# A two-layer macaron transformer on one core: the token mixer's attention in a written order that three engines keep

## The chip, the core and the metric

The kernel runs on one core of a Trainium2 chip. The metric is the device time of one execution in microseconds (us), as the median of several runs. A difference of about 0.3% (3 us here) is what a measurement of this kernel can tell from no change.

The core's engines are called PE (matrix products; PEld are its weight loads), DVE (vector), ACT (activation functions), POOL and SP (which issues the loads). Each works through its own list of instructions in order and waits at an instruction until what it needs has been done on the other engines.

## The reference

Two layers, each a half-weighted gated FFN, a token mixer and a second half-weighted gated FFN, on 256 tokens of width 1024, in fp32:

```python
for l in range(DEPTH):
    x = x + FFN_RES_WEIGHT * swiglu_ffn(x, ffn1_norm[l], ffn1_w1[l], ffn1_w3[l], ffn1_w2[l])
    h = rms_norm(x, mix_norm[l])
    (fq, fk, fv, ff, gu, gv, nq, nkc, nvc, nks, nvs, nkw, nvw, ng, pz) = split_mixing_columns(h @ w_in[l])
    ...
    o_a = fox_mixer(...)      # 4 heads, softmax(q k / 8 + c_i - c_j), c the running sum of log sigmoid(ff)
    o_b = gmlp_mixer(...)     # gelu(u) * (causal 128x128 mix of normalized gelu(v))
    o_c = nsa_mixer(...)      # 4 heads on one KV head: compressed, selected and window branch, gated
    o_d = pool_mixer(...)     # causal averages over 2, 4, 8, 16 tokens, then a 64x64 product
    x = x + jnp.concatenate([o_a, o_b, o_c, o_d], axis=-1) @ w_out[l]
    x = x + FFN_RES_WEIGHT * swiglu_ffn(x, ffn2_norm[l], ffn2_w1[l], ffn2_w3[l], ffn2_w2[l])
```

With 256 tokens the NSA selection takes all four blocks and the window spans everything, so those two branches are plain causal attention over different keys and values.

## The kernel before

All products with weights are made in two parts to keep fp32 precision: a matrix is loaded (L109), its rounded part `h` is made by ACT (L112) and the rest `lo` by DVE (L113). Such a pair is called a split here. `mm3` (L133 to L135) makes a product from three passes, `mm2` (L139, L140) from two. One 128x2048 weight tile is split in two halves of 128x1024, or in four of 128x512 for the first tiles of an FFN. Four tiles hold loaded weights (`raws`), four pairs hold split ones (`spl`), eight PSUM banks hold products.

An FFN is a loop over 22 up tiles and 8 down columns of 22 products each; PE works there without a break. The mixer is a list of calls (L820 to L888) whose steps are short and depend on each other:

- projections A, U, D, C, B, Z (`project`, `u_proj`, `z_proj`), each with its splits;
- six attention jobs of one pair of heads: F0 and F1 (forget attention), N0 to N3 (two pairs by two branches of NSA). A job is `scores` (8 products L750; DVE adds the mask and takes the maximum, L758; ACT takes exponentials and sums, L760), `weights` (DVE inverts the sums, L766 and L768, and scales the rows, four times L772; PE transposes, six times L775; ACT copies them out, L777) and `values` (8 products, L787);
- the compressed branch: `cmp_hidden` (four calls, L444), `cmp_gelu`, `cmp_out`, `cmp_keys`, `cmp_scores` (L707, then the sum with the mask on DVE, L710, and a softmax), `cmp_weights` (L732); its product with the values is L793 in `done`;
- the gate (`gate_mix`, L550 to L558) and the pools (`pool_mix`, `pool_out`; L593, evacuated by L127 on ACT and L128 on DVE);
- the output projection `out_part`: four generators w00, w01, w10, w11 of 16 steps with 3 products each, called in pieces by `fill` between the other steps.

The order of the calls is not the order on the engines: a list scheduler works out, when the kernel is built, which ready instruction each engine takes next, from its own estimate of times. What comes out is a fixed list for each engine. The call order serves as priority. So a split whose tile is loaded is put wherever the scheduler thinks ACT and DVE are free, also between the steps of a job.

"Attention" below is the stretch from the running sums of the forget gate (`forget_sums`, L663) to `done`; "layer 0" and "layer 1" are its two occurrences.

Of the kernel before, what the change touches and what calls it, by code (L numbers as in the profile page):

```python
# [21 lines left out]
F32 = mybir.dt.float32  # L22
# [48 lines left out]
def tile_macaron(ctx, tc, xT, g0, const0, consts, params, w13, w2, wA, wB, wD, wC, wE, wcmp, wo, out):  # L71
# [27 lines left out]
    def halves(s):  # L99
        return s.rearrange("p (a n) -> p a n", a=2)  # L100

# [237 lines left out]
    def mixer(l, norm, par):  # L339
# [6 lines left out]
        e = SimpleNamespace()  # L346
# [10 lines left out]
        def project(wg, n):  # L357

            ps = [bank_a(), bank_a()]
            for q in range(2):  # L360
                h, lo = split(wg[q], 4 * n)
                for kk in range(4):
                    k = 4 * q + kk
                    s = slice(n * kk, n * kk + n)
                    for t in range(2):
                        tok = slice(128 * t, 128 * t + 128)
                        mm3(ps[t][:, :n], (xs[k][0][:, tok], xs[k][1][:, tok]), (h[:, s], lo[:, s]), k == 0, k == 7)
            return ps
# [34 lines left out]
        def a_proj():  # L403
            e.pA = project(wA[l], 384)
# [46 lines left out]
        def cmp_gelu():  # L451

            x = bank_h()[:, 0:64].rearrange("p (a h n) -> p a h n", a=2, h=2)[:, :, :, 0:NC]
            for a in range(2):
                for hb in range(2):
                    nc.tensor.matmul(x[:, a, hb, :], e.hid[a][:, 128 * hb:128 * hb + 128], C("stack")[:, 0:NC],
                                     start=True, stop=True)
            g = w1p.tile([128, 2, 2, 16], F32, name="g")[:, :, :, 0:NC]
            nc.scalar.activation(g, x, AF.Square)
# [3 lines left out]
            nc.scalar.activation(g, g, AF.Exp, scale=-1.5957691216057308)  # L463
            nc.vector.tensor_scalar(g, g, 1.0, None, op0=ALU.add)
# [10 lines left out]
        def cmp_out():  # L475
# [14 lines left out]
            kiv = inv_rms(kss[0:NC, :], 64, 1, NC)  # L490
            nc.vector.scalar_tensor_tensor(kcn[0:NC, 0:64], pkc[0:NC, 0:64], kiv, Pm("kcn", NC), op0=ALU.mult,
# [71 lines left out]
        def z_proj():  # L563
            h, lo = split(wE[l, 1], 2048)
            pz = halves(bank_h())
            for t in range(2):
                tok = slice(128 * t, 128 * t + 128)
                for k in range(8):
                    s = slice(256 * k, 256 * k + 256)
                    mm3(pz[:, t, :], (xs[k][0][:, tok], xs[k][1][:, tok]), (h[:, s], lo[:, s]), k == 0, k == 7)  # L570
            z = halves(s2())
            for t in range(2):
                nc.scalar.activation(z[:, t, :], pz[:, t, :], AF.Copy, scale=e.rstd[:, t:t + 1])
            e.z = z
# [23 lines left out]
        def b_proj():  # L598
            e.pB = project(wB[l], 384)
# [33 lines left out]
        def d_proj():  # L633
            e.pD = project(wD[l], 400)
# [35 lines left out]
        def fox_bias(pair):  # L670
# [10 lines left out]
            e.bias = [(b0[:, i, 0:128], b1[:, i, :]) for i in range(2)]  # L681


        def c_proj():
            e.pC = project(wC[l], 512)
# [16 lines left out]
        def cmp_scores():  # L702
# [11 lines left out]
            sc8 = sc.rearrange("p t h n -> p (t h) n")[:, :, 0:NC]  # L714
            cmx = wk.tile([128, 8], F32)
            nc.vector.tensor_reduce(cmx, sc8, op=ALU.max, axis=AX.X)
            nc.vector.tensor_tensor(sc8, sc8, cmx.unsqueeze(2).to_broadcast([128, 8, NC]), op=ALU.subtract)
            nc.scalar.activation(sc8, sc8, AF.Exp)
            csm = wk.tile([128, 8], F32)
# [22 lines left out]
        def scores(jb):  # L742

            q, ks = jb.qk()
            if jb.branch is None:
                fox_bias(jb.pair)
# [5 lines left out]
            bias = e.bias if jb.branch is None else [(mask[:, 128:256], mask)] * 2  # L752
# [10 lines left out]
        def weights(jb):  # L763
# [5 lines left out]
            jb.pT = []  # L769
            for i in range(2):  # L770
                for t, c in enumerate(tcols):
                    nc.vector.tensor_scalar(jb.s[i][:, c], jb.s[i][:, c], rv[:, t, i:i + 1], None, op0=ALU.mult)  # L772
                p = bank_h()
# [31 lines left out]
        def out_part(d, q, accs):  # L805

            h, lo = split(wo[l, d, q], 2048)
            for c, kk in [(c, kk) for k2 in (0, 2) for c in range(4) for kk in (k2, k2 + 1)]:
# [22 lines left out]
        c_proj()  # L831
        c_stats()
        forget_sums()
        b_proj()
        c_post()
        b_stats()
        cmp_hidden(0, 0)
        c_heads()
        scores(F0)
        b_post()  # L840
        z_proj()
        scores(F1)
        cmp_hidden(0, 1)
        weights(F0)
        gate_mix()
        cmp_hidden(1, 0)
        b_heads()
        pool_mix()
        values(F0)
        scores(N0)  # L850
        weights(F1)
        cmp_hidden(1, 1)
        pool_out()
        done(F0)
        scores(N1)
        cmp_gelu()
        values(F1)
        done(F1)
# [3 lines left out]
        weights(N0)  # L862
        fill(w00, 4)
        cmp_out()
        scores(N2)
        values(N0)
        fill(w00, 4)
        weights(N1)
        fill(w00)
        cmp_keys()  # L870
        scores(N3)
        values(N1)
        fill(w01, 4)
        weights(N2)
        cmp_scores()
        fill(w01, 4)
# [4 lines left out]
        weights(N3)  # L881
        fill(w10, 6)
        cmp_weights()
        fill(w10)
        values(N3)
        done(N1)
        done(N3)
        fill(w11, 8)  # L888

# [131 lines left out]
```

## Time and profile before

| | us |
|---|---|
| median of 3 runs | 983.67 (982.35 to 985.51) |
| the profiled execution | 980.94 |
| its span, first to last instruction | 979.2 |
| PE busy | 966.6 (99%) |
| DVE busy | 696.7 (71%) |
| ACT busy | 531.8 (54%) |
| weights and data loaded | 179.28 MB |

PE's busy time is a sum over pipelined products with modelled ends, so 99% does not mean that PE streams at full rate all the time; idle time of PE, and stretches in which its clock is lower, are read separately. The clock is granted at two levels, 1.2 and 2.4 GHz, shown as 0.50 and 1.00.

### The profile page before, as it was taken

The numbers are of one execution on the slowest core, as the hardware profiler recorded it, in microseconds if no ns is written. First come the engines' busy times: TensorE is split into PE (matmuls) and PEld (weight loads), VectorE is DVE, ScalarE is ACT, GpSimd is POOL, SyncE is SP. The second block draws the span as 40 slices with busy tenths as digits, with TensorE's granted clock in tenths as the row PEclk, the third lists the DMA queues.
The fourth block names the chain that finished last, engine by engine and source line by source line (L and its number), as shares of the span: only waits on it lengthen the run. The fifth ranks groups of instructions, "written<-read, shape, count | busy, mean of one in ns | idle before, by whom it ended". The sixth has DMA issues, their size and how long they took to land.

```text
span 979.2 us, 14917 instructions
## 1 busy us (share of the span) xinstructions
PE 966.6 (99%) x5840; PEld 840.3 (86%) x5840; DVE 696.7 (71%) x1256; ACT 531.8 (54%) x969; POOL 65.1 (7%) x67
## 2 busy tenths in 40 slices
PE   8999999999999999999999999999999999999998
PEld 6888888898779888888888888888987788888887
DVE  5988776575857777776668777665758587777751
ACT  6656555453746555654445655544537475565530
POOL 2000000032002000000010000001220030000000
PEclk9999999999979999999999999999999999999999
DMA  8975554535634655555545555545437255555530
GB/s 302 327 250 193 179 208 151 183 134 202 221 124 150 236 174 184 201 175 182 205 172 178 204 178 178 199 162 173 173 130 282 74 205 172 186 201 173 177 108 17
DMA packets 28150, 179.28 MB, mean 183 GB/s; under 512 B 3248, under 2 KB 5168, under 8 KB 8240
## 3 DMA queue, kind: packets, MB, share of 16 engines
q1 hardware_dynamic: 27792, 178.19, 52.3%
q8 instruction: 46, 0.75, 0.3%
q10 hardware_dynamic: 288, 0.14, 0.1%
q14 instruction: 24, 0.20, 0.1%
HBM read 177.27 MB, written 1.05 MB: 182 GB/s over the span
## 4 chain that ended last, share of the span: by engine, by line
PE 91%; ACT 3%; DMA 3%; DVE 3%; issue 1%; POOL 0%; SPq 0%; POOLq 0%
PE h L139 32%; PE a L139 17%; PE h L140 16%; PE a L140 8%; PE a L133 4%; PE a L135 4%; PE a L134 4%; DMA r<-in_wo_dram 2%; ACT h L112 1%; DVE lo L113 1%; DMA x<-in_xT_dram 1%; PE h L775 1%; PE a L787 1%; ACT s L760 1%; DVE s L758 0%
## 5 line engine op out<-in xcount | busy, mean ns | idle before, releaser
L113 DVE TENSOR_TENSOR lo<-r,h 128x1024 fp32r<-128x1024 f32 (+4 forms) x346 | 392.4, 1148 | 163.7 <-ACT h L112 163.0
L139 PE MATMUL h<-hl,h 128*128 128x512 f32 x1408 | 496.8, 398 | 1.7 <-ACT h L112 1.2
L112 ACT ACTIVATE h<-r 128x1024 fp32r<-128x1024 f32 (+4 forms) x346 | 328.6, 974 | 273.9 <-issue 227.1
L140 PE MATMUL h<-hl,lo 128*128 128x256 f32 x1408 | 395.0, 281 | 0.4 <-DVE lo L113 0.2
L139 PEld LDWEIGHTS h<-hl,h 128*128 128x128 f32 x1408 | 264.2, 188 | 66.4 <-ACT h L112 1.7
L140 PEld LDWEIGHTS h<-hl,lo 128*128 128x128 f32 x1408 | 265.8, 189 | 1.9 <-DVE lo L113 1.9
L139 PE MATMUL a<-hl,h 128*128 128x512 f32 x704 | 247.6, 397 | 0.0
L140 PE MATMUL a<-hl,lo 128*128 128x256 f32 x704 | 197.0, 280 | 0.0
L139 PEld LDWEIGHTS a<-hl,h 128*128 128x128 f32 x704 | 132.1, 188 | 32.6 <-DVE hl L125 1.0
L140 PEld LDWEIGHTS a<-hl,lo 128*128 128x128 f32 x704 | 132.8, 189 | 0.0
L224 DVE SCALAR_TENSOR_TENSOR x<-a,x 128x256 f32<-128x256 f32 x80 | 32.9, 421 | 51.7 <-PE a L140 46.0
L294 DVE TENSOR_TENSOR s<-h,s 128x256 f32<-128x256 f32 x176 | 66.0, 416 | 1.1 <-ACT s L293 1.1
L295 DVE TENSOR_TENSOR s<-s,rb 128x512 f32<-128x512 f32 x88 | 60.9, 692 | 2.8
L293 ACT ACTIVATE s<-h 128x256 f32<-128x256 f32 x176 | 56.5, 371 | 2.7 <-PE h L140 2.7
L124 ACT ACTIVATE hl<-s 128x256 fp32r<-128x256 f32 x92 | 38.2, 417 | 34.4 <-DVE s L298 34.2
L201 POOL TENSOR_TENSOR s<-s 128x512 f32<-128x512 f32 x12 | 16.8, 1399 | 594.9 <-ACT s L197 594.9
L297 ACT ACTIVATE s<-s 128x256 f32<-128x256 f32 x88 | 35.5, 403 | 17.9 <-DVE s L295 17.8
L133 PE MATMUL a<-h,hl 128*128 128x384 f32 (+2 forms) x128 | 45.2, 353 | 0.0
L135 PE MATMUL a<-h,hl 128*128 128x384 f32 (+2 forms) x128 | 44.9, 351 | 0.0
L134 PE MATMUL a<-lo,hl 128*128 128x384 f32 (+2 forms) x128 | 44.9, 351 | 0.0
L125 DVE TENSOR_TENSOR hl<-s,hl 128x256 fp32r<-128x256 f32 x92 | 38.4, 419 | 2.5 <-ACT hl L124 2.5
L298 DVE TENSOR_TENSOR s<-s 128x256 f32<-128x256 f32 x88 | 36.9, 419 | 3.4 <-ACT s L297 3.4
(186 smaller groups left out, 791.0 us busy)
## 6 DMA issues: line engine op xcount, KB each, us to landing
r<-in_w_dram SPq DMA_DIRECT2D x129, 1024.0 KB, 4.9
r<-in_wcmp_dram SPq DMA_DIRECT2D x8, 1024.0 KB, 4.8
r<-in_wo_dram SPq DMA_DIRECT2D x8, 1024.0 KB, 6.7
r<-in_wE_dram SPq DMA_DIRECT2D x4, 1024.0 KB, 5.0
r<-in_wC_dram SPq DMA_DIRECT2D x4, 1024.0 KB, 4.7
r<-in_wD_dram SPq DMA_DIRECT2D x4, 800.0 KB, 4.4
r<-in_wA_dram SPq DMA_DIRECT2D x4, 768.0 KB, 4.3
r<-in_wB_dram SPq DMA_DIRECT2D x4, 768.0 KB, 4.3
```

The source lines that it names most:

```text
L112: nc.scalar.activation(h[:, c], r[:, c], AF.Copy)
L113: nc.vector.tensor_tensor(lo[:, c], r[:, c], h[:, c].bitcast(F32), op=ALU.subtract)
L124: nc.scalar.activation(th, src, AF.Copy)
L125: nc.vector.tensor_tensor(tl, src, th.bitcast(F32), op=ALU.subtract)
L133: nc.tensor.matmul(o, wgt[0], mov[0], start=start, stop=False)
L134: nc.tensor.matmul(o, wgt[0], mov[1], start=False, stop=False)
L135: return nc.tensor.matmul(o, wgt[1], mov[0], start=False, stop=stop)
L139: nc.tensor.matmul(o, wgt[0], mov[2], start=start, stop=False)
L140: return nc.tensor.matmul(o[:, :T], wgt[1], mov[0], start=False, stop=stop)
L293: nc.scalar.activation(hr[:, j, :], st[m][j][:, T:], AF.Copy)
L294: nc.vector.tensor_tensor(hr[:, j, :], st[m][j][:, :T], hr[:, j, :], op=ALU.add)
L295: nc.vector.tensor_tensor(hr, hr, st["rb"].unsqueeze(1).to_broadcast([128, 2, T]), op=ALU.mult)
```

## The change

The mixer's call order from the running sums to the last output steps is rewritten, some steps are cut into pieces, and the order of the calls is made the order of the instructions on PE, DVE and ACT: `pin` links each instruction of this stretch to the one before it on its engine. SP and POOL are not linked, nor is what comes ahead of the stretch or behind it; instructions of the following FFN can still be placed between linked ones.

- `project`, `z_proj` and `out_part` first issue their splits and pause (`yield`), so the caller says at which place in the order the splits stand and where the products follow. In the old code B's products stood in one piece; now they come in quarters with other steps between.
- `weights` is cut into `scale` (DVE) and `trans` (PE transposes, ACT copies); a job's `scale` now stands with the next job's `scores`, before or after it, and its `trans` some steps later.
- `fox_bias` is called by itself; `cmp_gelu`, `cmp_out` and `cmp_scores` pause between their parts; `cmp_gelu` copies its product out of PSUM once (one more small ACT instruction), and `z_proj` uses one bank for each half of the tokens instead of one for both.

No product is added or removed: PE has as many instructions as before, ACT has two more in all, DVE as many.

```diff
+    def pin(start):
+        last = {}
+        for i in list(nc.cur_bb.bb.instructions)[start:]:
+            if i.engine in (mybir.EngineType.PE, mybir.EngineType.DVE, mybir.EngineType.Activation):
+                if i.engine in last:
+                    tc.add_manual_dep(i, last[i.engine], mybir.DependencyInfo(mybir.DependencyClass.NoSync,
+                                                                             mybir.DependencyReason.DATA), reason="pin")
+                last[i.engine] = i.name
...
+        def project(wg, n, ps):
+            hl = [split(wg[q], 4 * n) for q in range(2)]
+            yield
+            for k in range(8):
...
+                if k % 2:
+                    yield
...
-        def weights(jb):
+        def scale(jb):
...
+        def trans(jb):
...
         def out_part(d, q, accs):
             h, lo = split(wo[l, d, q], 2048)
+            yield
...
+        bq, zq = b_proj(), z_proj()
+        go = lambda gen: next(gen, None)
+        go(bq)
         c_stats()
         forget_sums()
+        here = len(nc.cur_bb.bb.instructions)
+        go(bq)
+        gate_mix()
+        go(bq)
+        go(zq)
+        cmp_hidden(0, 0)
         c_post()
+        fox_bias(0)
+        go(bq)
         c_heads()
...
+        done(F0)
+        trans(F1)
         fill(w00, 4)
+        go(gelu)
+        pool_out()
+        go(w01)
+        values(F1)
+        scale(N0)
+        scores(N1)
+        done(F1)
         fill(w00, 4)
+        go(gelu)
+        trans(N0)
+        fill(w00, 4)
+        values(N0)
+        scale(N1)
+        scores(N2)
         fill(w00, 4)
+        outs = cmp_out()
+        go(outs)
...
+        go(w10)
+        trans(N1)
+        fill(w01, 4)
+        go(outs)
+        values(N1)
+        scale(N2)
+        scores(N3)
+        fill(w01, 4)
+        trans(N2)
+        cmp_keys()
         fill(w10, 4)
         values(N2)
+        cs = cmp_scores()
+        go(cs)
+        go(w11)
+        scale(N3)
+        fill(w10, 4)
+        go(cs)
+        trans(N3)
+        fill(w10, 3)
+        go(cs)
+        fill(w10, 2)
         cmp_weights()
+        values(N3)
         fill(w10)
         done(N1)
         done(N3)
         fill(w11, 8)
+        pin(here)
```

Line numbers of the new kernel differ: L123 is the DVE half of a split (before L113), L122 its ACT half (L112), L793 the scaling (L772), L788 and L790 the inverted sums (L766, L768), L780 the masked maximum (L758), L782 the exponentials (L760), L800 the transposes (L775), L802 their copies (L777), L732 the masked compressed scores (L710), L137 and L138 the evacuation of the pools (L127, L128), L135 the DVE half of a finished head pair (L125).

The first place is DVE around the scaling of the last job, N3 (in the rows `rv` is the inverted sum, `s` a job's scores, `sc` the compressed scores, `lo<-r,h` a split). Before, layer 0:

```order
L766 RECIPROCAL rv<-sm 128x4
L768 TENSOR_TENSOR rv<-rv,gate 128x4
L772 TENSOR_SCALAR s<-s,rv 128x128
L772 TENSOR_SCALAR s<-s,rv 128x256
L710 TENSOR_TENSOR sc<-h,cst 128x8x15
L772 TENSOR_SCALAR s<-s,rv 128x128
L716 TENSOR_REDUCE cmx<-sc 128x8
L772 TENSOR_SCALAR s<-s,rv 128x256
```

Half of the scaling stands ahead of the masked compressed scores and no split between them. On DVE now:

```order
L732 TENSOR_TENSOR sc<-h,cst 128x8x15
L123 TENSOR_TENSOR lo<-r,h 128x1024 x2
L788 RECIPROCAL rv<-sm 128x4
L123 TENSOR_TENSOR lo<-r,h 128x512
L790 TENSOR_TENSOR rv<-rv,gate 128x4
L123 TENSOR_TENSOR lo<-r,h 128x512
L793 TENSOR_SCALAR s<-s,rv 128x128
L793 TENSOR_SCALAR s<-s,rv 128x256
L793 TENSOR_SCALAR s<-s,rv 128x128
L793 TENSOR_SCALAR s<-s,rv 128x256
```

The scaling of N3 now stands behind the masked compressed scores, both halves of w11's split and two quarters of the next FFN's first split.

The second place is DVE around the scaling of N0 (`hl<-h,par,hl` is the evacuation of the pools). Before, layer 0:

```order
L113 TENSOR_TENSOR lo<-r,h 128x1024 x2
L448 COPY s<-h 128x256
L766 RECIPROCAL rv<-sm 128x4
L768 TENSOR_TENSOR rv<-rv,gate 128x4
L128 SCALAR_TENSOR_TENSOR hl<-h,par,hl 128x256
L772 TENSOR_SCALAR s<-s,rv 128x128
L772 TENSOR_SCALAR s<-s,rv 128x256
L772 TENSOR_SCALAR s<-s,rv 128x128
L772 TENSOR_SCALAR s<-s,rv 128x256
```

Two halves of a split stand ahead of the scaling here too, but ahead of the pools' evacuations. On DVE now:

```order
L138 SCALAR_TENSOR_TENSOR hl<-h,par,hl 128x256 x2
L123 TENSOR_TENSOR lo<-r,h 128x1024 x2
L788 RECIPROCAL rv<-sm 128x4
L790 TENSOR_TENSOR rv<-rv,gate 128x4
L793 TENSOR_SCALAR s<-s,rv 128x128
L793 TENSOR_SCALAR s<-s,rv 128x256
L793 TENSOR_SCALAR s<-s,rv 128x128
L793 TENSOR_SCALAR s<-s,rv 128x256
```

The scaling of N0 now stands behind both evacuations of the pools and both halves of w01's split.

The third place is ACT from the evacuation of the pools to the copies of N0's transposed weights. Before, layer 0:

```order
L127 ACTIVATE hl<-h,par 128x256
L112 ACTIVATE h<-r 128x1024
L127 ACTIVATE hl<-h,par 128x256
L124 ACTIVATE hl<-a 128x256
L459 ACTIVATE g<-h 128x4x15
L112 ACTIVATE h<-r 128x1024 x2
L760 ACTIVATE s,sm<-s,nm 128x128
L760 ACTIVATE s,sm<-s,nm 128x256
L760 ACTIVATE s,sm<-s,nm 128x128
L760 ACTIVATE s,sm<-s,nm 128x256
L124 ACTIVATE hl<-a 128x256
L777 ACTIVATE s<-h 128x384 x2
```

On ACT now:

```order
L137 ACTIVATE hl<-h,par 128x256 x2
L122 ACTIVATE h<-r 128x1024 x2
L782 ACTIVATE s,sm<-s,nm 128x128
L782 ACTIVATE s,sm<-s,nm 128x256
L782 ACTIVATE s,sm<-s,nm 128x128
L782 ACTIVATE s,sm<-s,nm 128x256
L134 ACTIVATE hl<-a 128x256
L802 ACTIVATE s<-h 128x384 x2
```

The kinds of work and their sequence are much the same; which split it is has moved (two halves of w01 behind both evacuations), and so has what the exponentials wait for on DVE.

## Rows read from the trace of the kernel before

**Rows 1.** The profile page: TensorE's clock in 40 equal slices, in tenths of full speed.

```profile
PEclk9999999999979999999999999999999999999999
```

**Rows 2.** What PE waited for in layer 0's attention: us in total, times, longest.

```profile
PE h L775 <- DVE s L772: 1.6, 2, 1.3
PE h L750 <- ACT s L629: 0.6, 1, 0.6
PE a L787 <- ACT s L777: 0.5, 1, 0.5
```

**Rows 3.** The same for layer 1's attention.

```profile
PE h L775 <- DVE s L772: 1.7, 2, 1.3
PE a L787 <- ACT s L777: 0.4, 1, 0.4
```

**Rows 4.** Stretches with a low clock: length, then busy time by engine; PEclk third from last.

```profile
278.80:289.60 10.80, 10.44 (x50) 8.14 (x51) 7.26 (x33) 4.15 (x15) 0.00 (x0) 0.53 0.29 99
...
763.60:767.40 3.80, 3.80 (x18) 2.07 (x17) 2.85 (x15) 2.07 (x9) 0.00 (x0) 0.55 0.00 0
```

**Rows 5.** PE in order of time, layer 0: start, length; idle time before in brackets.

```profile
229.31 0.28 PE L663 MATMUL h<-lf,c0t 128*128 128x4 f32 x2
...
258.22 0.93 PE L750 MATMUL h<-s 64*128 64x128 f32 x8 [0.61 <-ACT s L629]
259.08 0.88 PE L775 MATMUL h<-c0t,s 128*128 128x128 f32 x6
...
264.81 0.28 PE L134 MATMUL a<-hl,h 128*128 128x256 f32 x1
264.93 0.28 PE L135 MATMUL a<-hl,lo 128*128 128x256 f32 x1
...
275.88 0.87 PE L787 MATMUL a<-s 128*64 128x256 f32 x8
276.68 0.55 PE L775 MATMUL h<-c0t,s 128*128 128x128 f32 x3
278.51 0.30 PE L775 MATMUL h<-c0t,s 128*128 128x128 f32 x1 [1.28 <-DVE s L772]
...
296.17 1.13 PE L793 MATMUL a<-pcT,vbd 128*128 128x256 f32 x4
```

**Rows 6.** PE in order of time, layer 1.

```profile
714.65 0.28 PE L663 MATMUL h<-lf,c0t 128*128 128x4 f32 x2
...
778.02 1.13 PE L793 MATMUL a<-pcT,vbd 128*128 128x256 f32 x4
```

**Rows 7.** DVE in order of time, layer 0.

```profile
254.24 0.75 DVE L555 TENSOR_TENSOR s<-h,par 128x256 f32<-128x256 f32 x2
...
260.30 2.35 DVE L113 TENSOR_TENSOR lo<-r,h 128x1024 fp32r<-128x1024 f32 x2
...
263.84 1.00 DVE L772 TENSOR_SCALAR s<-s,rv 128x128 f32<-128x128 f32 x4
264.76 0.48 DVE L128 SCALAR_TENSOR_TENSOR hl<-h,par,hl 128x256 fp32r<-128x256 f32 x1
...
284.02 0.17 DVE L766 RECIPROCAL rv<-sm 128x4 f32<-128x4 f32 x1
...
284.43 0.55 DVE L772 TENSOR_SCALAR s<-s,rv 128x128 f32<-128x128 f32 x2
...
296.07 1.90 DVE L113 TENSOR_TENSOR lo<-r,h 128x512 fp32r<-128x512 f32 x3 [6.83 <-ACT h L112]
```

**Rows 8.** ACT in order of time, layer 0.

```profile
256.50 0.71 ACT L124 ACTIVATE hl<-s 128x256 fp32r<-128x256 f32 x2
...
258.54 2.01 ACT L112 ACTIVATE h<-r 128x1024 fp32r<-128x1024 f32 x2
260.44 0.40 ACT L760 ACTIVATE s<-s,nm 128x128 f32<-128x128 f32 x1
...
262.19 0.86 ACT L777 ACTIVATE s<-h 128x384 f32<-128x384 f32 x2
```

More of the change, by code (lines that the diff above doesn't have):

```diff
@@ L569, in z_proj @@
                     s = slice(256 * k, 256 * k + 256)
[L570 to L574, printed above, removed]
+                    mm3(pz, (xs[k][0][:, tok], xs[k][1][:, tok]), (h[:, s], lo[:, s]), k == 0, k == 7)
+                nc.scalar.activation(e.z[:, t, :], pz, AF.Copy, scale=e.rstd[:, t:t + 1])
+                yield
         def pool_mix():
@@ L680, in fox_bias @@
             nc.vector.tensor_tensor(b1, p, mask.unsqueeze(1).to_broadcast([128, 2, 256]), op=ALU.add)
-            e.bias = [(b0[:, i, 0:128], b1[:, i, :]) for i in range(2)]
+            e.bias[pair] = [(b0[:, i, 0:128], b1[:, i, :]) for i in range(2)]
         def c_proj():
-            e.pC = project(wC[l], 512)
+            e.pC = projected(wC[l], 512)
         def c_stats():
@@ L744, in scores @@
             q, ks = jb.qk()
-            if jb.branch is None:
-                fox_bias(jb.pair)
             s = [bank_h(), bank_h()]
@@ L751, in scores @@
                                      start=True, stop=True)
-            bias = e.bias if jb.branch is None else [(mask[:, 128:256], mask)] * 2
+            bias = e.bias[jb.pair] if jb.branch is None else [(mask[:, 128:256], mask)] * 2
             jb.s = [s2(), s2()]
@@ L772, in weights @@
                     nc.vector.tensor_scalar(jb.s[i][:, c], jb.s[i][:, c], rv[:, t, i:i + 1], None, op0=ALU.mult)
+        def trans(jb):
+            jb.pT = []
+            for i in range(2):
                 p = bank_h()
@@ L843, in mixer @@
[L843 to L858, printed above, removed]
         wacc = [halves(bank_a()), halves(bank_a())]
         w00, w01 = out_part(0, 0, wacc), out_part(0, 1, wacc)
-        fill(w00, 4)
-        weights(N0)
-        fill(w00, 4)
@@ L864, in mixer @@
-        cmp_out()
+        go(w00)
+        go(bq)
+        cmp_hidden(0, 1)
+        b_stats()
+        scores(F0)
+        go(zq)
+        fox_bias(1)
+        cmp_hidden(1, 0)
+        scale(F0)
+        b_post()
+        scores(F1)
+        go(zq)
+        trans(F0)
+        b_heads()
+        cmp_hidden(1, 1)
+        pool_mix()
+        scale(F1)
+        scores(N0)
+        values(F0)
+        gelu = cmp_gelu()
+        go(gelu)
+        done(F0)
+        trans(F1)
+        fill(w00, 4)
@@ L865, in mixer @@
+        go(gelu)
[5 more added lines that the diff above has]
+        done(F1)
+        fill(w00, 4)
+        go(gelu)
+        trans(N0)
+        fill(w00, 4)
+        values(N0)
+        scale(N1)
         scores(N2)
-        values(N0)
         fill(w00, 4)
[L868 to L876, printed above, removed]
+        outs = cmp_out()
```

54 lines of the change are left out of this document (26 added, 28 removed).

## The prediction

> **What bounds the kernel now.** I looked at the clock row of the page first [rows 1]: full speed everywhere except around slices 11 and 12, and those slices lie in layer 0's attention. Then at what PE waited for inside the two attentions: 1.6 + 0.6 + 0.5 = 2.7 us in layer 0 [rows 2] and 1.7 + 0.4 = 2.1 us in layer 1 [rows 3], 4.8 us in all. Then at the clock in short stretches [rows 4]: 10.8 us at a mean of 0.53 in layer 0, 3.8 us at 0.55 in layer 1. Outside these two stretches PE streams, and no order can give it back anything. So the reader should see a kernel bound by PE, in which a new order of the attentions can win at most these waits and the low clock.
>
> What the low clock costs: from the forget sums to the last product of the compressed branch layer 0 takes 296.17 - 229.31 = 66.9 us [rows 5] and layer 1 takes 778.02 - 714.65 = 63.4 us [rows 6], with the same instructions. Of the 3.5 us between them 0.6 are waits, so the longer low stretch costs 2.9 more. In layer 1 the clock was at 1.2 GHz for about 3.8 x (1 - 0.55) / 0.5 = 3.4 us; half of that, with 0.4 us of waiting in it taken out first, is 1.5. So the clock costs 1.5 + 4.4 = 5.9 us. (From layer 0's stretch alone: 10.2 us low, half is 5.1 instead of 4.4.) All that can be won is 4.8 + 5.9 = 10.7 us.
>
> **The change part by part.** Nothing changes on PE but the order; a product of 256 columns follows the last at 0.12 us [rows 5], so four steps of `out_part` (12 products) are 1.45 us, eight score products 0.86, eight value products 0.80, six transposes 0.8. The order on the three engines is now fixed, and what matters is which DVE or ACT work stands ahead of something that PE needs. I walked the new lists by hand, with these lengths: two halves of a split take 2.0 us on ACT [rows 8] and 2.3 on DVE, a quarter 0.6, four scalings 1.0, inverse and gate 0.4 until the first scaling [rows 7]; four exponentials 1.75 and a pair of copies 0.86 [rows 8]. The same six waits come in both layers, since the lists are the same there.
>
> (e) *The scaling of N3*, the dearest. When PE ends the compressed scores, DVE adds their mask (about 0.2), then makes both halves of w11 (2.3), the inverse, two quarters of the next FFN's split (1.2) and only then scales; with some 0.3 for the small steps, 0.28 for the first scaling and 0.14 for the hand-over, the first transpose can start 4.4 us after the scores. PE has four output steps until then, 1.45 us. Wait: 3.0, and 0.1 more for the second head. If the two quarters were done earlier it would be 1.9. In the old order half of N3's scaling stood ahead of the compressed scores, and no split behind them.
>
> (b) *The scaling of N0.* From the end of `pool_out`: ACT evacuates one half (0.48), DVE its rest (0.48), ACT the second half; then ACT splits w01 (2.0), DVE follows 1.15 behind, then inverse and scaling. The second head's transposes end 6.6 us after `pool_out`; PE needs 0.80 + 0.86 + 1.45 + 0.8 = 3.9 for what stands between. Wait 2.7; if ACT's second evacuation need not let DVE's first go ahead, 2.0. The trace doesn't settle it, because in the old order a split stood between the two on ACT. I take 2.4, the middle. On why they may alternate, the Trainium skill's page "PSUM — Partial Sum Buffer" (section "PSUM bank collisions raise a hardware error") says that two engines may not read one bank in the same partitions at once. By that rule the wait is 2.7 and the sum 0.6 us larger; no row here shows such a collision.
>
> (c) *The values of N0.* N1's exponentials now stand ahead of N0's copies on ACT, and they wait for N1's maxima, which stand behind N0's scaling: 0.3 + 1.75 + 0.3 + 0.4 = 2.8 us after the scaling. PE's transposes end 0.4 behind the scaling and four output steps take 1.45. Wait: 0.9.
>
> (a) *The head transposes of C.* `c_post` now stands behind the gate's five DVE instructions and Z's split. From the end of the gate's products: 0.75 [rows 7], about 0.7 for the product with u, 0.7 on ACT [rows 8], a split of which DVE ends some 3.3 us after ACT began, 0.6 for the first norm: 6.2 us. PE has two quarters of B, 24 products of 384 columns, by width 0.18 each, and two small groups of 0.5 to 1.0: 5.8. Wait 0.4, and 0.6 later the second half: 1.0 in all.
>
> (d) *The values of N1*: w10's split (2.0) stands ahead of the copies on ACT; 3.0 us against 0.8 + 1.45 on PE, about 0.6. (f) *The compressed weights*: the softmax of the compressed scores stands behind N3's scaling, in between two more quarters; 2.9 against 2.25 on PE, 0.65. Three more places come out at 0.15 to 0.45 us each, below what this walk can tell; I take them at nothing and keep 0.85 for the upper end.
>
> Sum of waits: 1.0 + 2.4 + 0.9 + 0.6 + 3.1 + 0.65 = 8.65 us in each attention, 17.3 in the kernel, 12.5 more than before.
>
> *The clock.* Before, it fell in both attentions just after one wait of 1.28 us among small products [rows 4, 5], and not after 0.61. Waits (b) and (e) are longer, so I expect it to fall twice in each attention. I price a fall by the shorter stretch, 3.4 us low or 1.7 lost, less what it hides of the next wait (0.9 for c, 0.65 for f): 0.8 + 1.05 = 1.85 in each attention, 3.7 in all, against 5.9 before. The bounds are nothing, and four falls of the longer kind (below).
>
> *Beside it.* The extra ACT copy in `cmp_gelu`, 60 columns twice in the kernel, stands where ACT waits for DVE anyway; a second bank for Z costs no instruction. On SP one output weight is now loaded ahead of three compressed weights; its buffer is freed by B's split, long before. I price these at nothing; were that load late, `cmp_hidden` would wait behind it, a few tenths. POOL's work isn't moved. The FFNs keep their order.
>
> The sum: +12.5 - 5.9 + 3.7 = +10.3 us. On the profiled execution, 980.94 (span 979.2), that gives 991.2; that execution lies 2.7 us under the median of the runs, 983.67, so for the median I say 994.0.
>
> **The rivals.** *Not slower: the two splits reach nobody.* If PE comes to (b) and (e) later than I count, both of which are splits put straight ahead of a scaling, these waits go (11.0 us) and with them the falls of the clock (3.7): +10.3 - 14.7 = -4.4, so 979.3. For it: in the old list of DVE split halves stood ahead of N0's scaling too, and the longest wait was 1.28 us [rows 5]. Against it: the new splits begin only behind something that PE has just finished, so PE's own lateness moves them along. It decides where waits and clock together fall below 10.7 us.
>
> *No change.* The waits are some 60% of my count, 10.4, and the clock falls once in each attention, 2.0 in all instead of 5.9: +5.6 - 3.9 = +1.7, so 985.4.
>
> *A clock that stays low.* Each of the four falls lasts as long as that of layer 0: 4 x 5.1 - 2 x 1.55 (hidden waits) = 17.3 instead of 3.7: +23.9, so 1007.6. For it: layer 0's stretch lasted through dense output steps [rows 4]. Against it: layer 1's ended after a third of that. The Trainium skill's page "TensorE: Matmul & The Clock Gate" (section "A second HAM failure mode: psum-queue depth-cycling") says that many short pauses between groups of products can make the clock go up and down; by that rule this rival is the rule's own result, and rows 4 agree with it in kind: the clock fell in a stretch of short groups.
>
> **How the numbers follow.** The forecast, waits near my count and a clock that falls and soon returns: 0.60, between 987 and 1002. No change: 0.16. Splits that reach nobody: 0.14. A clock that stays low: 0.10. About 0.3%, 3 us, is what a measurement can tell from no change, so faster is 0.14, within it 0.16, slower 0.60 + 0.10 = 0.70. The low bound of the waits (a 0.5, b 2.0, c 0.4, d 0.2, e 1.9, f 0: 5.0 in each) with a clock that never falls gives 10.0 - 4.8 - 5.9 = -0.7, so 983; the upper waits (9.8 in each) with two long and two short falls give some +20, so 1004. The range is 982 to 1003; it leaves out the splits that reach nobody and the upper part of the low clock, about 0.2 together.
>
> **What would show it.** In the trace of the changed kernel PE's waits inside an attention should be led by the transposes (now L800) waiting for the scaling (L793): about 3 us ahead of N3's and 2 to 2.7 ahead of N0's, in both layers; then values (L812) waiting for copies (L802), 0.5 to 1 us. The clock should show 0.5 behind both. Right about N3 is who sees DVE make four split pieces between the masked compressed scores (L732) and N3's scaling with PE idle beside it. I am wrong if PE's waits in an attention sum to under 5 us, if the clock stays full, or if the FFNs change their time.

## The result, and the profile after

The changed kernel takes 990.25 us (986.36 to 992.76, 10 runs); the kernel before, run beside it on the same chip, 983.07 us (979.19 to 985.51). The ratio is 1.0075, 95% interval 1.0055 to 1.0096: 7.2 us slower, where 994.0 us was forecast. The profiled execution of the changed kernel has a span of 988.6 us, 9.4 us more than that of before.

Where the 9.4 us lie can be read from two lines of code: the forget sums (L685) open each attention's fixed stretch on PE, the product of the compressed branch (L818) closes it. These are the changed kernel's rows for the two lines; the last two times are the first and the last start.

```profile
L685 PE MATMUL h<-lf,c0t x4: 168/210/253, 230.4 to 718.3; 128*128 128x4 f32 x4
L818 PE MATMUL a<-pcT,vbd x8: 377/378/379, 300.1 to 788.2; 128*128 128x256 f32 x8
```

Layer 0's attention takes 300.1 - 230.4 = 69.7 us, 2.8 more than before [rows 5]; layer 1's, from the last start of the one to the last of the other, 69.9, 5.8 more than the 64.1 that the same reckoning gives for before. That makes 8.6 of the 9.4 us; 1.1 us lie ahead of the first attention, and the rest of the kernel is as before within 0.3 us. The 1.1 us can't be put down to the change: the stretch up to the first forget sum lies ahead of the fixing and takes between 227.9 and 232.3 us in the profiled executions of this document. So the place is the one that was forecast. What PE waited for there, layer 0 first, then layer 1 (us in total, times, longest), beside [rows 2, 3]:

```profile
PE h L800 <- DVE s L793: 4.9, 2, 2.7
PE h L756 <- DVE pcm L749: 0.6, 1, 0.6
PE h L415 <- DVE s L406: 0.6, 2, 0.4
PE a L812 <- ACT s L802: 0.4, 1, 0.4
PE h L772 <- ACT s L651: 0.4, 1, 0.4
PE h L604 <- ACT s L594: 0.2, 1, 0.2
...
PE h L800 <- DVE s L793: 4.9, 2, 2.7
PE a L812 <- ACT s L802: 1.3, 2, 0.9
```

In layer 1 the three rows L415, L772 and L604 come again with the same numbers. 7.1 and 7.4 us, against 2.7 and 2.1 before: the transposes (L800) waiting for the scaling (L793) lead in both layers. In order of time (start, length, idle time before in brackets) the two waits of layer 0 and the two of layer 1 are:

```profile
270.76 1.16 PE L800 MATMUL h<-c0t,s 128*128 128x128 f32 x6 [2.28 <-DVE s L793]
294.24 1.16 PE L800 MATMUL h<-c0t,s 128*128 128x128 f32 x6 [2.67 <-DVE s L793]
...
758.57 1.16 PE L800 MATMUL h<-c0t,s 128*128 128x128 f32 x6 [2.28 <-DVE s L793]
781.53 1.59 PE L800 MATMUL h<-c0t,s 128*128 128x128 f32 x6 [2.67 <-DVE s L793]
```

And DVE ahead of the second of them, N3's: the masked compressed scores (L732), both halves of w11's split, two quarters of the next FFN's split, and only then the scaling.

```profile
290.09 0.28 DVE L732 TENSOR_TENSOR sc<-h,cst 128x120 f32<-128x120 f32 x1 [3.31 <-PE h L729]
290.29 2.35 DVE L123 TENSOR_TENSOR lo<-r,h 128x1024 fp32r<-128x1024 f32 x2
292.56 0.17 DVE L788 RECIPROCAL rv<-sm 128x4 f32<-128x4 f32 x1
292.65 0.66 DVE L123 TENSOR_TENSOR lo<-r,h 128x512 fp32r<-128x512 f32 x1
293.23 0.15 DVE L790 TENSOR_TENSOR rv<-rv,gate 128x4 f32<-128x4 f32 x1
293.30 0.68 DVE L123 TENSOR_TENSOR lo<-r,h 128x512 fp32r<-128x512 f32 x1
293.90 1.00 DVE L793 TENSOR_SCALAR s<-s,rv 128x128 f32<-128x128 f32 x4
```

The clock, in stretches of 2 us (PEclk is third from last), after the first wait of layer 0 and around the end of the second of layer 1:

```profile
272.00:274.00 2.00, 2.00 (x12) 1.78 (x10) 0.70 (x5) 2.00 (x10) 0.00 (x0) 0.57 1.02 434
274.00:276.00 2.00, 1.85 (x11) 1.21 (x10) 1.86 (x10) 0.54 (x2) 0.00 (x0) 0.57 0.09 33
...
780.00:782.00 2.00, 0.47 (x2) 0.39 (x3) 2.00 (x8) 0.00 (x0) 0.00 (x0) 0.72 0.56 106
782.00:784.00 2.00, 2.00 (x12) 2.00 (x11) 1.97 (x7) 0.79 (x3) 0.00 (x0) 0.50 0.99 418
784.00:786.00 2.00, 2.00 (x17) 1.76 (x18) 0.82 (x4) 0.54 (x2) 0.00 (x0) 0.93 0.55 123
```

One fall in each attention, each (1 - PEclk) / 0.5 of these stretches, so 3.4 us at 1.2 GHz. In layer 0 that is 1.7 us lost. In layer 1 it is less: of the stretch from 780 to 782 us 1.1 us were low, and PE began only at 781.53, so the clock fell some 0.65 us before the wait ended, where it costs nothing, and about 1.4 us were lost. Behind the other two long waits the clock stayed at 1.00. The page's clock row is all nines now: against [rows 1] the clock got better, and the kernel slower.

### The profile page after: what moved, and what is told of

Read it like the earlier page. It is cut to its first block, busy times and chain, and to the rows that moved or that the text cites. A ratio compares the mean times of both kernels' runs of the same rounds, so it can differ in the third digit from the quotient of the medians.

```text
span 988.6 us, 14921 instructions
## 1 busy us (share of the span) xinstructions
PE 965.9 (98%) x5840; PEld 839.9 (85%) x5840; DVE 698.8 (71%) x1256; ACT 530.3 (54%) x971; POOL 65.9 (7%) x67
## 4 chain that ended last, share of the span: by engine, by line
PE 91%; DVE 5%; ACT 3%; DMA 1%; issue 0%; POOL 0%; SPq 0%; DVEq 0%; ACTq 0%
PE h L149 33%; PE h L150 17%; PE a L149 17%; PE a L150 8%; PE a L143 3%; PE a L144 3%; PE a L145 3%; DVE lo L123 2%; PE a L812 1%; ACT s L782 1%; ACT h L122 1%; DMA r<-in_w_dram 1%; PE h L143 1%; DVE s L793 1%; PE h L772 1%; PE h L144 1%
## 5 line engine op out<-in xcount | busy, mean ns | idle before, releaser
L123 DVE TENSOR_TENSOR lo<-r,h 128x1024 fp32r<-128x1024 f32 (+4 forms) x346 | 391.6, 1147 | 161.9 <-ACT h L122 161.4
L122 ACT ACTIVATE h<-r 128x1024 fp32r<-128x1024 f32 (+4 forms) x346 | 327.7, 974 | 265.8 <-issue 224.4
L135 DVE TENSOR_TENSOR hl<-s,hl 128x256 fp32r<-128x256 f32 x92 | 38.3, 418 | 3.5 <-ACT hl L134 3.5
L782 ACT ACTIVATE s<-s,nm 128x128 f32<-128x128 f32 (+1 forms) x48 | 21.3, 444 | 34.2 <-DVE nm L780 34.2
```

Source lines behind the costliest of these rows:

```text
L122: nc.scalar.activation(h[:, c], r[:, c], AF.Copy)
L123: nc.vector.tensor_tensor(lo[:, c], r[:, c], h[:, c].bitcast(F32), op=ALU.subtract)
L135: nc.vector.tensor_tensor(tl, src, th.bitcast(F32), op=ALU.subtract)
```

## The experiments

The forecast says that the waits come from splits queued ahead of what PE needs. Against it stands the thought that fixing the order costs by itself, wherever the splits stand. All kernels of this section have the changed kernel's parts, except where it is said. The table has every run: the median, the ratio to the kernel before on the same chip, the lengths of the two attentions in the profiled execution as reckoned above, and the sum of PE's waits in layer 0's attention. The kernel before took 980.3 to 982.2 us beside the later runs, so the ratios compare best. An attention's length is that of one execution, which can lie some us from the median (984.49 us for "w01's split later"). Where the expectations speak of the gate projection they mean Z, which the pools read.

| kernel | us | ratio (95%) | attentions, us | waits, us |
|---|---|---|---|---|
| before | 983.07 | 1 | 66.9, 64.1 | 2.7 |
| changed | 990.25 | 1.0075 (1.0055 to 1.0096) | 69.7, 69.9 | 7.1 |
| w11's split later | 993.50 | 1.0123 (1.0103 to 1.0144) | 70.7, 72.3 | 8.5 |
| w01's split later | 990.94 | 1.0096 (1.0068 to 1.0124) | 69.3, 69.9 | 7.4 |
| both later | 992.17 | 1.0117 (1.0098 to 1.0137) | 70.4, 71.9 | 8.3 |
| order not fixed | 964.28 | 0.9835 (0.9814 to 0.9856) | 58.5, 59.5 | 0.2 |
| before, order fixed | 1031.09 | 1.0528 (1.0489 to 1.0568) | 87.1, 87.9 | 19.3 |
| w01's split early | 985.82 | 1.0041 (1.0016 to 1.0066) | 68.3, 68.3 | 6.4 |
| w10's and w11's early | 988.31 | 1.0084 (1.0051 to 1.0118) | 68.4, 69.8 | 6.9 |
| all three early | 984.31 | 1.0037 (1.0012 to 1.0062) | 67.3, 68.2 | 5.8 |
| split pieces by table | 972.45 | 0.9911 (0.9879 to 0.9942) | 60.9, 61.4 | 1.7 |
| ACT alone by table | 994.81 | 1.0140 (1.0104 to 1.0176) | 71.8, 72.2 | 9.1 |
| early, in two steps | 976.76 | 0.9952 (0.9933 to 0.9971) | 63.4, 63.9 | 3.7 |
| split pieces and ACT by table | 972.22 | 0.9923 (0.9889 to 0.9956) | 61.7, 62.3 | 2.0 |

### The splits one step later

```diff
 # w11's split later
-        go(w11)
         scale(N3)
+        go(w11)
...
 # w01's split later
-        go(w01)
         values(F1)
         scale(N0)
...
         trans(N0)
+        go(w01)
```

> One line moves: the scaling of N3 stands ahead of w11's split instead of behind it; everything else is the changed kernel. Theory (the wait of the transposes is the split queued ahead of the scaling on VectorE): PE's wait of 2.67 us ahead of N3's transposes goes in both layers, 5.3 us in all. The split then stands between the masked compressed scores and their maxima, so the wait for the compressed weights (0.6 us) may grow to 1 or 2 us per attention. Sum: 985 to 987 us where the changed kernel has 990.25. Rival 1 (fixing the order on three engines costs in itself, wherever the split stands): PE's waits come up at another line with the same sum and the time stays at 989.5 to 991. Rival 2 (the clock's falls and not the waits carry the loss): layer 1's fall of some 3.4 us at half speed stood behind N3's transposes and goes, 1.7 us, but layer 0's, behind N0's, stays: about 988.5 with the waits unchanged in sum.

> One line moves: w01's split stands behind the transposes of N0 instead of ahead of N0's scaling. Theory: the wait of 2.28 us ahead of N0's transposes falls by the split's ScalarE and VectorE pieces, to between 0 and 0.8 us (the pools' evacuations stay ahead of the scaling); the wait for N0's copies ahead of its values stays or grows to 1 us, since the split now stands ahead of those copies. Sum: 3 to 4.5 us less, and 1.7 us more where the clock's fall of layer 0, which stood behind this wait, goes: 984.5 to 987. Rival 1 (fixing the order costs in itself): 989.5 to 991. Rival 2 (the wait is the turn-taking of ScalarE and VectorE over the pools' evacuations, not the split): the wait keeps 1.5 us or more and the time is 988 to 990.

> Both moves together. Theory: the two gains add, since the two waits stand 23 us apart: 980.5 to 983.5, at or a little under the kernel before; the clock stays full through both attentions. Rival 1 (fixing the order costs in itself): 989 to 991. Rival 2 (a common bound behind both, such as VectorE's sum of work between N0 and N3, gives one wait back when the other goes): 985 to 987, as with one move alone.

All three were too hopeful: with w11's split moved the kernel is 0.5% slower still, with w01's there is no gain that can be told. PE's waits show why. First w11 later, then w01 later, both in layer 0, and of w01 later PE at N1's transposes and values:

```profile
PE h L756 <- DVE pcm L749: 3.7, 1, 3.7
PE h L800 <- DVE s L793: 2.3, 1, 2.3
...
PE a L812 <- ACT s L802: 2.9, 2, 2.0
PE h L800 <- DVE s L793: 2.7, 1, 2.7
...
PE h L800 <- DVE nm L780: 0.6, 1, 0.6
...
274.61 0.55 PE L800 MATMUL h<-c0t,s 128*128 128x128 f32 x3 [0.57 <-DVE nm L780]
278.62 1.24 PE L812 MATMUL a<-s 128*64 128x256 f32 x8 [2.04 <-ACT s L802]
```

N3's 2.67 us are gone, and the compressed weights (L756) now wait 3.75 instead of 0.59: the split stands in the softmax that they need. In layer 1 the waits are 7.6 us against 7.4, and what makes that attention longer is the clock, at 1.2 GHz for 10.2 us instead of 3.4. With w01 later N0's 2.28 us are gone, and its values still wait 0.82 for their copies (the split stands behind these on ACT, not ahead of them, as the expectation has it). The debt goes to N1: DVE's half of the split stands ahead of its scaling, its second three transposes wait 0.57 and its values (L812) 2.04 instead of 0.43. The cause of each wait was named rightly, but it is a debt that goes to the next in the queue. Written later, the splits cost what they cost before. That is also what the first rival of each run says in kind, so these three runs alone leave it standing.

### The order not fixed, and the kernel before with its order fixed

```diff
 # order not fixed: the changed kernel without
-        pin(here)
```

> The changed kernel without the fixing of the order: the same calls in the same order, the same edits of parts, but the scheduler sets the order on each engine. It then puts N3's scaling ahead of the masked compressed scores and the splits for the output weights earlier. Theory (what counts is where the splits stand in VectorE's queue, and the fixing makes the written order real): both waits shrink under 1 us and the time is 980 to 985. Rival (the loss is in the rewritten parts: the copy of the hidden values, the gate projection's two banks, more pieces): the waits ahead of N0's and N3's transposes go, others come, and the time stays within 2 us of the changed kernel's 990.25.

```diff
 # before, order fixed: the kernel before with the function pin(), and
         forget_sums()
+        here = len(nc.cur_bb.bb.instructions)
         b_proj()
...
         fill(w11, 8)
+        pin(here)
```

> The kernel before with nothing but the fixing of its own written order on the three engines added, over the same stretch of the attention. Its calls write each split directly ahead of the matmuls that read it. Theory (what counts is where a split stands in the queues, and the scheduler had moved these): PE waits a whole first piece, 2 to 4 us, at B's two halves, the gate projection and each of the four output splits, 15 to 25 us per attention: 1010 to 1035 where the kernel before has 981.6 to 983. Rival (the scheduler's order of the kernel before is close to its written one, and the loss of the changed kernel is in its rewritten parts): 980 to 988.

Without the fixing the same calls take 964.28 us, 2.4% less than the changed kernel and 1.65% less than the kernel before, beyond what any theory gave. PE's instruction order is the changed kernel's, but for seven of 5840 products whose records swap places within their group; otherwise only DVE's and ACT's differ. All that is left of PE's waits in layer 0's attention is

```profile
PE h L415 <- DVE nqk L641: 0.2, 1, 0.2
```

and the clock is at 1.000. The kernel before with its own written order fixed is 5.3% slower, as the theory had it. So the change is two things of opposite sign: the new calls and parts gain 1.65% where the scheduler may order DVE and ACT, and fixing that order costs 2.4%. The engines have as many instructions with the fixing as without (PE 5840, DVE 1256, ACT 971), so I look for the cost in the order. The scheduler places w10's split like this, ACT first and then DVE (w11's follows in the same manner, ACT at 256.14, DVE at 258.94):

```profile
248.21 2.00 ACT L122 ACTIVATE h<-r 128x1024 fp32r<-128x1024 f32 x2
...
253.91 1.22 DVE L123 TENSOR_TENSOR lo<-r,h 128x1024 fp32r<-128x1024 f32 x1
255.04 0.17 DVE L788 RECIPROCAL rv<-sm 128x4 f32<-128x4 f32 x1
255.13 1.19 DVE L123 TENSOR_TENSOR lo<-r,h 128x1024 fp32r<-128x1024 f32 x1
```

That is long ahead of the changed kernel's place (DVE at 280.52 for w10, 290.29 for w11), and ACT's half is done 3.7 us before DVE's begins.

### The splits earlier

```diff
 # w01's early
         cmp_hidden(0, 1)
+        go(w01)
         b_stats()
...
         pool_out()
-        go(w01)
...
 # w10's and w11's early (wacc1 is an empty list first, filled where the banks were taken)
         scores(F1)
+        wacc1 = []
+        w10, w11 = out_part(1, 0, wacc1), out_part(1, 1, wacc1)
+        go(w10)
         go(zq)
...
         scores(N0)
+        go(w11)
         values(F0)
```

> Only w01's split is written earlier, ahead of b_stats; w10's and w11's stay where the changed kernel has them. Theory (each late split is a wait of its own): the wait of 2.28 us ahead of N0's transposes goes and nothing takes its place, N3's 2.67 us stays; with the fall of the clock behind it in layer 0 (1.7 us) that is 990.25 less 4.6 to 6.3: 984 to 986. Rival (conserved: VectorE and ScalarE are a common bound from N0 to N3 and give the wait back behind N0, as when the split was moved later): 988 to 991.

> Only w10's and w11's splits are written earlier, behind scores(F1) and scores(N0); w01's stays. Theory: N3's wait of 2.67 us goes in both layers, and of the smaller waits (values of N1 0.4, compressed weights 0.6) up to 1 us per attention, and the fall of the clock behind N3 in layer 1 (1.7 us): 990.25 less 5.3 to 9: 981 to 985. The gains of this run and of the one with w01 alone should add up to that of the run with all three. Rival (conserved): 988 to 991; or w11's split, now written into the busy stretch ahead of N0, makes N0's wait longer by 1 to 2 us and gives back as much.

> The order stays fixed, TensorE's order stays that of the changed kernel row for row, and only the three splits of output weights are written earlier: w01's ahead of b_stats, w10's behind scores(F1), w11's behind scores(N0), each about where its buffer comes free, one lap of the pipeline ahead of the changed kernel. Theory now (the written splits stand too late, in the stretch in which VectorE and ScalarE have no slack; the fixing itself costs nothing): the waits ahead of N0's and N3's transposes (2.28 and 2.67 us) both go, PE's waits fall from 7 us to under 2.5 us per attention, the clock stays full, and the time is 968 to 974, most of the way to the unfixed order's 964.28. Rival 1 (the fixing costs in itself): 988 to 991. Rival 2 (what the scheduler gains is the interleaving of small pieces, not the splits): one wait moves to another line as in the last three runs, 984 to 991.

w01's split alone came out in the theory's range, 985.82 us: N0's wait is gone and N3's 2.67 us stay. But one of 1.1 us is new, ahead of the transposes of B's heads (L415). With the other two the theory failed: N3's wait is gone, N0's grew, as the rival says, and 988.31 us is no gain that can be told (1.0084 against 1.0075). All three take 984.31 us, no less than w01's alone as far as can be told (1.0037 against 1.0041); other waits took the place of those that went, as the second rival says. First w01's early, then w10's and w11's:

```profile
PE h L415 <- DVE nqk L641: 1.1, 1, 1.1
...
PE h L800 <- DVE s L793: 3.5, 1, 3.5
```

DVE with all three early, at w10's and at w11's pieces, and PE at the pools' product and at the transposes of N0:

```profile
260.21 2.36 DVE L123 TENSOR_TENSOR lo<-r,h 128x1024 fp32r<-128x1024 f32 x2 [2.04 <-ACT h L122]
...
268.18 2.36 DVE L123 TENSOR_TENSOR lo<-r,h 128x1024 fp32r<-128x1024 f32 x2 [2.04 <-ACT h L122]
...
261.54 0.32 PE L604 MATMUL h<-cst,s 128*64 128x128 f32 x1 [2.22 <-ACT s L594]
274.40 1.07 PE L800 MATMUL h<-c0t,s 128*128 128x128 f32 x6 [0.59 <-DVE s L793]
```

A split is two steps, ACT's and then DVE's, and one written place puts both at the same point of two fixed queues. ACT reached its half only behind F1's or N0's exponentials, DVE stood 2.04 us with nothing that its list let it do, and ACT's half held up Z's evacuation (L594), for which PE waited 2.22 us. The Trainium skill's page "PSUM — Partial Sum Buffer" (section "Engine vs sequencer instructions") calls these engines' queues strict FIFO; the first of the two rows agrees: DVE stood idle for 2.04 us, though PE had finished the products that DVE's next instruction copies (L464) 1.25 us before the wait ended.

### The pieces of the splits at the scheduler's places

With a table in place of the written order, DVE's and ACT's rows can be put where the scheduler has them without fixing, a kind at a time. First only the ten split pieces on each engine (Z, w00, w01, w10, w11), the rest in its written order; then ACT's queue alone, with DVE's as written; then the split pieces on DVE with all of ACT's queue.

```diff
 # pin() goes through a list for each engine instead of the written order
-        for i in list(nc.cur_bb.bb.instructions)[start:]:
+        for i in pe + [ve[k] for k in dve] + [sc[k] for k in act]:
```

> The order stays fixed, by a table: TensorE's as in the changed kernel, and on ScalarE and VectorE all work in its written order except the pieces of the five splits of the attention's second half (the gate projection's and the four output splits, ten pieces on each engine), which stand at the places in the two queues that the scheduler gives them in the kernel without fixing. There the ScalarE piece of a split stands many instructions ahead of its VectorE piece; one written place puts both at the same point, and in the run with all three splits early VectorE then stood idle 2.04 us ahead of w10's and of w11's pieces, waiting for ScalarE's. Theory (the places of the split pieces on each of the two queues are the whole of it): PE's waits under 1.5 us per attention, full clock, 964 to 970. Rival 1 (the interleaving of the other chains, as the scaling of N0 with the activation of the compressed hidden values, carries a part): one or two waits of about 1 us per attention stay, 970 to 980. Rival 2 (the split places bring no more than writing them early did): 980 to 986.

> The order stays fixed, by a table: TensorE's and VectorE's as in the changed kernel, ScalarE's as the scheduler has it without fixing, so that ScalarE's pieces of the splits come early and VectorE's stay where the changed kernel wrote them. Theory 1 (VectorE's pieces queued ahead of the scalings set the waits): N0's and N3's waits lose only what VectorE waited for ScalarE, at most 0.5 us each; time 986 to 991. Theory 2 (the wait of VectorE for ScalarE's pieces is what counts): both waits fall under 1 us, 975 to 982.

> The order stays fixed by a table: TensorE's and VectorE's as in the run with only the split pieces at the scheduler's places (972.45 us), ScalarE's wholly as the scheduler has it, so that also its copies and evacuations stand where the scheduler puts them, among F1's exponentials for instance. What is still open is which queue carries the 8 us between that run and the unfixed order (964.28). Theory (ScalarE: three of the four waits that are left there, 0.82, 0.38 and 0.33 us, are for ScalarE's copies): these go, PE's waits fall from 1.7 to under 0.5 us per attention, 965 to 969. Rival (VectorE's finer interleaving carries it, as the scaling of N0 among the activation's steps): the wait of 0.82 us for N0's copies stays, 970 to 973.

The split pieces alone bring 990.25 to 972.45 us: by the ratios 1.0075 - 0.9911 = 1.64% of the 2.40% that fixing cost, some 16 of 23.6 us. That is its first rival: two thirds of what the theory expected. What PE still waits for there in layer 0:

```profile
PE a L812 <- ACT s L802: 0.8, 1, 0.8
PE h L772 <- ACT s L651: 0.4, 1, 0.4
PE h L604 <- ACT s L594: 0.3, 1, 0.3
PE h L415 <- DVE nqk L641: 0.2, 1, 0.2
```

ACT's order alone gains nothing (994.81 us, above both expectations). ACT's pieces stand early there, but ACT waits for weights, at the first piece of w01's split:

```profile
248.72 1.06 ACT L122 ACTIVATE h<-r 128x1024 fp32r<-128x1024 f32 x1 [6.24 <-DMA r<-in_wo_dram]
```

The same piece waited 1.59 us without fixing. Its load waits on SP's queue. Here are DVE's half of w00's split and the first load behind it, w01's, with ACT alone by table, and behind the dots with the order not fixed:

```profile
241.42 2.35 DVE L123 TENSOR_TENSOR lo<-r,h 128x1024 fp32r<-128x1024 f32 x2
243.84 6.61 SPq L119 DMA_DIRECT2D r<-in_wo_dram  x3
...
231.18 2.38 DVE L123 TENSOR_TENSOR lo<-r,h 128x1024 fp32r<-128x1024 f32 x2 [0.26 <-ACT h L122]
236.64 11.80 SPq L119 DMA_DIRECT2D r<-in_wo_dram  x3
```

With ACT alone by table the load is issued 0.07 us after w00's half on DVE is done, 7.2 us later than without fixing. So DVE's late halves keep the loaded weights in their buffers (four, `raws`), and the next load back. I read this as the cause; no run changed the buffers, and none moved DVE's halves alone. By this reading both halves have to be early. And ACT's order together with the split pieces adds nothing (972.22 us): the wait of 0.83 us for N0's copies stays, as the rival says. ACT's and POOL's lists in this trace are those of the kernel without fixing, instruction for instruction, and PE's but for a few neighbours in a group; only DVE's differs. So the last 8 us should hang on the finer order of DVE's other work. Without fixing DVE starts N0's scaling (L793, at 262.12) before the pools' first evacuation (L138, at 263.13), for which it has to wait, and here behind both. Which rows carry how much wasn't separated, and no run fixed the scheduler's whole order, so that fixing by itself costs nothing is not shown.

### Early and in two steps, written by hand

```diff
 # in out_part: a step of its own for each engine
-            h, lo = split(wo[l, d, q], 2048)
-            yield
+            for c in (slice(0, 1024), slice(1024, 2048)):
+                nc.scalar.activation(h[:, c], r[:, c], AF.Copy)
+            yield
+            for c in (slice(0, 1024), slice(1024, 2048)):
+                nc.vector.tensor_tensor(lo[:, c], r[:, c], h[:, c].bitcast(F32), op=ALU.subtract)
+            yield
...
 # ACT's step, and DVE's: w01 ahead of b_stats, behind scores(F0);
 # w10 behind the first step of zq, behind scores(F1); w11 behind b_heads, behind scores(N0)
```

> The order stays fixed as written, no table: the split of the output weights gets two steps, ScalarE's pieces and VectorE's pieces, and the calls place them apart, as the scheduler does: w01 ahead of b_stats and behind scores(F0), w10 behind the first gate step and behind scores(F1), w11 behind b_heads and behind scores(N0). The gate projection's and w00's pieces stay together. Theory (early, and ScalarE's half ahead of VectorE's): 964 to 972, near the run with the table. Rival (the gate projection's and w00's places, or other interleaving, carry a part): 974 to 982. If it falls in with the run that only wrote the splits early: 982 to 986.

976.76 us, in the rival's range: 0.5% faster than the kernel before with a fixed order and no table, against 0.4% slower with the same splits early but in one step. Two steps are worth 0.85% here, some 8 us; ACT's halves of w10 and w11 also stand earlier than there. The version that beats both kernels by most is the changed kernel with its order left free, 964.28 us.

## Why the prediction was right

**The place and the kind** were right: PE's waits in the attentions, led by the transposes, with the split pieces of (b) and (e) on DVE just ahead of the scaling, and the FFNs unchanged. The sum is near too, in part by luck. Waits of 14.5 us less 4.8 are +9.7. The clock costs 3.1 us, and in the kernel before it cost 6.6: the low stretches there are 10.2 and 3.4 us long, and 0.36 us of waiting lie in the first. (The forecast has 5.9. It takes 0.4 us of waiting out of the second, in which none lies: the clock was back at 767.24, and PE's next wait began at 767.47.) Together that is +6.2 us, where the attentions grew by 8.6. The other 2.4 us were not forecast: groups behind a wait also take longer, six transposes 1.16 us against 0.82 to 0.88 with no wait, eight value products 1.23 against 0.87, some 0.3 us at each. Forecast was +10.3, with the waits counted too long and this left out.

**The terms.** (a) the heads of C: 1.0 forecast, 0.6 measured. (b) N0's scaling: 2.4, measured 2.28 in both layers. ACT's second evacuation did wait for DVE's first, as the upper bound had it:

```profile
265.75 0.48 DVE L138 SCALAR_TENSOR_TENSOR hl<-h,par,hl 128x256 fp32r<-128x256 f32 x1 [1.54 <-ACT hl L137]
...
266.27 0.47 ACT L137 ACTIVATE hl<-h,par 128x256 fp32r<-128x256 f32 x1 [0.55 <-DVE hl L138]
266.78 0.48 DVE L138 SCALAR_TENSOR_TENSOR hl<-h,par,hl 128x256 fp32r<-128x256 f32 x1 [0.54 <-ACT hl L137]
```

So the turn-taking that the forecast set beside the rule of the Trainium skill's page "PSUM — Partial Sum Buffer" (section "PSUM bank collisions raise a hardware error") is there. The rows agree with the rule in that the program makes ACT wait for DVE; no run shows a collision. The 2.7 us reckoned with it were 0.4 too many all the same; which other length of that walk was too long I didn't look for. (c) N0's values: 0.9, measured 0.88 in layer 1, and in layer 0 hidden behind the slow clock. (d) N1's values: 0.6 (its own numbers give 3.0 - 0.8 - 1.45 = 0.75), measured 0.43. (e) N3's scaling: 3.1, measured 2.67. (f) the compressed weights: 0.65, measured 0.59 in layer 0 and none in layer 1, behind the slow clock. Of three small places, which it doesn't name, it took the waits at nothing; two more waits show, 0.4 and 0.2. Together 17.3 forecast, 14.5 measured; (a) and (e), and (c) and (f) where the slow clock hid them, are most of the difference.

**The clock** was forecast to fall behind both long waits of each attention, at 3.7 us with what it hides taken out. It fell at one of the two in each, and hid (c) in layer 0 and (f) in layer 1. So the term was too large. Reckoned as in the forecast, two falls at 1.7 and 1.4 us less the 0.9 and 0.6 that they hid are 1.6 us, not 3.7, and the waits with those two are 16.0 us, not 17.3. The rival of a clock that stays low, 1007.6 us, didn't come: each fall ended after 3.4 us. The Trainium skill's page "TensorE: Matmul & The Clock Gate" (section "A second HAM failure mode: psum-queue depth-cycling") describes a clock that goes up and down; here it did so once in 70 us.

**Where it was wrong:** the sentence that all that an order can win is 4.8 + 5.9 = 10.7 us. The unfixed kernel's attentions take 58.5 + 59.5 us against 66.9 + 64.1, 13.0 less, and its time is 1.65%, 16 us, under the kernel before. The bound has the low clock at 5.9 where it cost 6.6, and it takes PE's busy time as fixed. Since 0.7 us of waits are left in the unfixed kernel, some 2.3 us must have come out of the busy time. One part is seen: the 64 products of `cmp_hidden` in an attention, at full clock in both kernels, take 4.9 us in the kernel before (L444) and 4.3 in the unfixed one (L460). Another may be that a group whose input comes in pieces waits inside itself, and that is counted as busy, as with the six transposes above; how the rest divides wasn't looked for. The rival "the splits reach nobody" (979.3) was the nearest to what this order of calls can give, and still 15 us short. The forecast also didn't ask what fixing takes away: it read the new lists as the change, and never compared them with those that the scheduler makes of the same calls.

## What to carry over

When a change rewrites the calls and fixes their order at once, run it once without the fixing: here the rewriting was worth -1.65% and the fixing +2.4%, and the sum hid both. A step that passes through two engines wanted two places in two fixed queues here, the first engine's well ahead of the second's, and about when its buffer comes free; moving such a step later along a tight chain only sent the wait to whoever stood next. Before a wait is booked as a gain, name the row that becomes late when it goes.

## What was unexpected of the hardware

The same wait doesn't always bring the clock down. PE's 2.28 us ahead of N0's transposes, with the same work on both sides, was followed by 3.4 us at 1.2 GHz in layer 0 and by none in layer 1; with N3's 2.67 us it was the other way round, and there the clock fell before the wait had ended. In this execution a wait of this length came at half a fall; what decides between the two was not found. The number of falls isn't fixed either: the mean granted clock of the ten executions lies between 0.992 and 0.997, by my estimate some 16 and 6 us at 1.2 GHz ((1 - clock) / 0.5 of 988 us). The execution with 0.992 took 989.67 us and two with 0.997 some 991, so the times don't follow the clock in these.
